# Scattering one dense tile's expert gates with single-element indirect DMAs, and selecting per head over all four tiles

## The chip, the cores and the metric

The kernel runs on one core of a Trainium2 chip. The metric is the device time of one execution in microseconds, the median of several runs. Beside the times there is one profiled execution, from which all rows below come; its own time is given with its span.

## The reference

The reference is a decoder trunk of two layers over 512 tokens of 1024 channels, with 16 meta tokens ahead of them. The first layer mixes by causal pooling, the second by stick-breaking attention; both are followed by a PEER expert network, and this is what the change is about:

```python
s = einsum('bthpc,hpnc->bthpn', q, sub_keys)          # 8 heads, 2 halves, 128 keys each
top_s, top_i = top_k(s, 16)
cand_s = top_s[..., 0, :, None] + top_s[..., 1, None, :]
best_s, best_pos = top_k(cand_s as 256 candidates, 16)
expert = top_i0 * 128 + top_i1 of best_pos             # one of 16384
gate = softmax(best_s)
act = gelu(hx . u[expert]);  y = sum(gate * act * v[expert])
```

So each token takes 8 x 16 experts, and adds their `v` rows, weighted by gate times gelu of the token's product with their `u` rows.

## The kernel before, in words

The 512 tokens are four tiles of 128. In each layer's `peer` (line 255) tiles 0 to 2 are **dense**: every one of the 16384 experts is multiplied with all 384 tokens, in 128 blocks j of 128 experts. A **u step** (`u_parts`, line 307) computes a block's activations with 24 matmuls of 384 columns (line 314; float32 is split into a high and a low half, three products for each of 8 chunks), and the gelu of it (line 321). A **v step** (`v_step`, line 660) multiplies activations by gates (line 678), splits the product and the block's `v` into halves (lines 675 to 683) and adds into six banks `y` with 18 matmuls of 512 columns (line 690). The gates of a block come from a DRAM tensor `gout`, 32 tokens to a group, read by line 673 for four blocks at once. Tile 3 is **gathered**: for each of its 128 expert slots an indirect DMA (`fetch`, line 340) brings one row of `u` and `v` per token, 1 MB in all, VectorE takes the product (line 355), ScalarE its gelu (line 359), VectorE adds the weighted `v` (line 367). In the first layer 16 more such rows serve the meta tokens, behind the others. That makes 144 and 128 rows.

Each layer goes through three stages:

- The **query stage** (loop over heads, line 496): two query projections per head (weights "w"), products with the keys (line 521), and `top16` (line 391) of 8 score vectors per token tile pair on VectorE, five passes each. `select` (line 399) then picks the best 16 of 80 candidates for the gathered tile, one head at a time. `plan` (lines 474 to 487) strews u steps between the heads: it adds WQ_DVE per head to one clock, WQ_PE to another, and inserts u steps of 3.91 us (`ucost`) until the second has caught up.
- The **build stage** (`gate_stream`, line 606): per dense tile one `select` over its eight heads, then `build_gates` (line 553): 32 blocks of 4 tokens, each with four VectorE one-hot passes (lines 593 to 596), 8 matmuls (lines 574 and 576) and one eviction on ScalarE (line 581), stored to `gout`. u steps, in four parts, are put between them by cost (lines 622 to 639). Their activations are spilled to `aout` and read back later.
- The **value stage** (`order`, line 646): the remaining u steps (kept in SBUF), and 128 v steps; while u steps last the order is one u step and two v steps, then v steps alone.

Rows of the gathered tile run through all three by `row_step`, four steps to a row (fetch, product, gelu, update, with up to three rows in flight). The loops call it against a clock: in the value stage

```python
                    tu += ucost
                    while tr < tu and row_step():
                        tr += ROW_PERIOD[layer][1] / 8
                while row_step():
                    pass
```

so a row takes 4 x 13.5/8 = 6.75 us of a clock that runs 3.91 us for each u or v step, and what is left runs after the last of them. Behind it come `finish` for the gathered tile, the last two v steps' matmuls and the additions of `y`.

The tile framework orders each engine's instructions by program order and readiness in a plan made ahead; on the chip each engine takes them in that order. `issue_after` pins: row products and updates stand on VectorE behind the last low half that the program has made before them (`vmark`), their gelus behind the last ScalarE high half (`amark`). The low halves of u and w weights (`load_w`, line 274) are made on GpSimd until the build stage begins and on VectorE from there (`gating`).

After the first layer's experts, `attention` takes the tiles in the order 3, 0, 1, 2 and then the meta tokens (line 765).

## Time and profile before

| | us |
|---|---|
| median of 3 runs | 3131.46 |
| lowest, highest | 3129.51, 3134.83 |
| profiled execution, its own time | 3127.99 |
| its span, first to last instruction | 3126.3 |

The 1.7 us between the last two lie around the program. The median is 3.5 us above the profiled execution. Times in rows are counted from the span's start; PE is TensorE's matmuls, DVE VectorE, ACT ScalarE, POOL GpSimd, SP SyncE. The matmuls of one group overlap, so their mean durations are longer than their distance.

### The profile page before, as it was taken

The numbers are of one execution on the slowest core, as the hardware profiler recorded it, in microseconds if no ns is written. First come the engines' busy times: TensorE is split into PE (matmuls) and PEld (weight loads), VectorE is DVE, ScalarE is ACT, GpSimd is POOL, SyncE is SP. The second block draws the span as 40 slices with busy tenths as digits, with TensorE's granted clock in tenths as the row PEclk, the third lists the DMA queues.
The fourth block names the chain that finished last, engine by engine and source line by source line (L and its number), as shares of the span: only waits on it lengthen the run. The fifth ranks groups of instructions, "written<-read, shape, count | busy, mean of one in ns | idle before, by whom it ended". The sixth has DMA issues, their size and how long they took to land.

```text
span 3126.3 us, 45813 instructions
## 1 busy us (share of the span) xinstructions
PE 2999.0 (96%) x16514; PEld 2671.7 (85%) x16514; DVE 2449.1 (78%) x5636; ACT 1354.3 (43%) x2184; POOL 688.7 (22%) x704
## 2 busy tenths in 40 slices
PE   8988999999999999999999989799999999999999
PEld 7887988988888888879965778798898888888887
DVE  3999998878777778786456469999987777777765
ACT  3443645643333333335455334354655333333333
POOL 3431311111111111114245244222110111111100
PEclk9999999999999999999999999999999999999999
DMA  3435877799989899762100344477878998989875
GB/s 134 179 121 202 282 265 265 274 360 329 338 312 321 314 329 329 273 245 90 55 1 1 108 177 144 158 262 269 303 253 326 358 314 321 331 308 333 307 250 164
DMA packets 286708, 758.52 MB, mean 243 GB/s; under 512 B 23184, under 2 KB 176784, under 8 KB 248336
## 3 DMA queue, kind: packets, MB, share of 16 engines
q1 hardware_dynamic: 222544, 390.92, 36.8%
q0 software_dynamic: 39168, 285.23, 24.9%
q10 hardware_dynamic: 24768, 79.44, 6.6%
q8 instruction: 129, 2.11, 0.3%
q14 instruction: 99, 0.81, 0.1%
HBM read 673.99 MB, written 81.53 MB: 242 GB/s over the span
## 4 chain that ended last, share of the span: by engine, by line
PE 77%; DVE 16%; DMA 3%; ACT 2%; issue 1%; POOL 0%; SPq 0%; DVEq 0%; ACTq 0%; POOLq 0%
PE y L690 31%; PE psu L314 27%; PE pg L574 3%; PE pg L576 3%; PE pp L124 2%; PE pp L125 2%; PE pp L123 2%; DVE mr L395 1%; DVE prod L355 1%; DVE w_lo L281 1%; DMA gt<-gout 1%; DVE ti L397 1%; DVE hx L367 1%; DMA w<-in_peer_ut_dram 1%; DVE ti L394 1%
## 5 line engine op out<-in xcount | busy, mean ns | idle before, releaser
L343 POOL DMA_INDIRECT row<-in_peer_uv_dram,ei x272 | 383.3, 1409 | 1833.1 <-DVE hx L367 1481.9
L314 PE MATMUL psu<-n_hi,w_lo 128*128 128x384 f32 x2048 | 701.5, 343 | 42.4 <-DVE w_lo L281 39.9
L314 PE MATMUL psu<-n_hi,w_hi 128*128 128x384 f32 x2048 | 720.4, 352 | 11.5 <-ACT ac L321 7.2
L314 PE MATMUL psu<-n_lo,w_hi 128*128 128x384 f32 x2048 | 703.0, 343 | 0.6 <-DVE n_lo L118 0.6
L279 ACT ACTIVATE w_hi<-w 128x1024 fp32r<-128x1024 f32 x288 | 305.6, 1062 | 467.7 <-PE psu L314 373.2
L690 PE MATMUL y<-v_lo,wt_hi 128*128 128x512 f32 x1536 | 473.6, 390 | 1.6 <-DVE v_lo L676 1.6
L690 PE MATMUL y<-v_hi,wt_hi 128*128 128x512 f32 x1536 | 473.8, 390 | 0.5 <-ACT v_hi L675 0.5
L690 PE MATMUL y<-v_hi,wt_lo 128*128 128x512 f32 x1536 | 473.6, 389 | 0.0
L314 PEld LDWEIGHTS psu<-n_hi,w_lo 128*128 128x128 f32 x2048 | 394.0, 192 | 49.0 <-DVE w_lo L281 45.8
L314 PEld LDWEIGHTS psu<-n_hi,w_hi 128*128 128x128 f32 x2048 | 395.4, 193 | 17.8 <-ACT ac L321 7.5
L314 PEld LDWEIGHTS psu<-n_lo,w_hi 128*128 128x128 f32 x2048 | 394.0, 192 | 5.5 <-DVE n_lo L118 1.1
L682 ACT ACTIVATE wt_hi<-wt 128x384 fp32r<-128x384 f32 x256 | 134.3, 525 | 574.0 <-PE y L690 295.5
L683 DVE TENSOR_TENSOR wt_lo<-wt,wt_hi 128x384 fp32r<-128x384 f32 x256 | 142.5, 557 | 264.3 <-ACT wt_hi L682 264.3
L281 DVE TENSOR_TENSOR w_lo<-w,w_hi 128x1024 fp32r<-128x1024 f32 x228 | 278.2, 1221 | 83.2 <-ACT w_hi L279 82.6
L690 PEld LDWEIGHTS y<-v_lo,wt_hi 128*128 128x128 f32 x1536 | 288.1, 188 | 63.3 <-DVE v_lo L676 2.9
L690 PEld LDWEIGHTS y<-v_hi,wt_lo 128*128 128x128 f32 x1536 | 288.3, 188 | 60.4
L355 DVE SCALAR_TENSOR_TENSOR prod<-row,hnat 128x1024 bf16<-128x1024 f32 x272 | 337.7, 1241 | 0.6 <-DMA row<-in_peer_uv_dram,ei 0.5
L367 DVE SCALAR_TENSOR_TENSOR hx<-row,gwt,hx 128x1024 f32<-128x1024 f32 x256 | 334.5, 1307 | 2.1
L690 PEld LDWEIGHTS y<-v_hi,wt_hi 128*128 128x128 f32 x1536 | 286.8, 188 | 52.8 <-ACT v_hi L675 0.9
L676 DVE TENSOR_TENSOR v_lo<-v,v_hi 128x1024 fp32r<-128x1024 f32 x256 | 312.2, 1219 | 5.4 <-ACT v_hi L675 5.2
L581 ACT ACTIVATE stage<-pg 128x512 f32<-128x512 f32 x192 | 216.9, 1137 | 149.2 <-PE pg L576 146.3
L675 ACT ACTIVATE v_hi<-v 128x1024 fp32r<-128x1024 f32 x256 | 270.8, 1058 | 10.6 <-DMA v<-in_peer_uv_dram 9.5
(313 smaller groups left out, 4695.0 us busy)
## 6 DMA issues: line engine op xcount, KB each, us to landing
w<-in_peer_ut_dram SPq DMA_DIRECT2D x256, 512.0 KB, 5.9
v<-in_peer_uv_dram SPq DMA_DIRECT2D x256, 512.0 KB, 6.1
gout<-stage ACTq DMA_DIRECT2D x24, 2048.0 KB, 8.4
gt<-gout SPq DMA_DIRECT2D x64, 768.0 KB, 10.2
aout<-ac ACTq DMA_DIRECT2D x148, 192.0 KB, 4.0
ac<-aout SPq DMA_DIRECT2D x148, 192.0 KB, 5.9
w<-in_peer_wq_dram SPq DMA_DIRECT2D x32, 512.0 KB, 3.4
wn<-in_w_kv_dram SPq DMA_DIRECT2D x8, 1024.0 KB, 5.5
```

The source lines that it names most:

```text
L279: amark.append(sc.activation(whi, w, AF.Copy))
L281: vmark.append(v.tensor_sub(wlo, w, whi.bitcast(F32)))
L314: m = pin(pe.matmul(ps[:, :ND], a[:, k, :], b[:, k, c0:c0 + ND], start=st, stop=en))
L343: gp.indirect_dma_start(out=row, out_offset=None, in_=peer_uv, in_offset=bass.IndirectOffsetOnAxis(ap=item[1], axis=0))
L355: v.scalar_tensor_tensor(prod, row[:, :D], 1.0, hn_nat[i], ALU.mult, ALU.mult, accum_out=dot)
L367: v.scalar_tensor_tensor(acc, row[:, D:], wt, acc, ALU.mult, ALU.add)
L581: sc.activation(stage[:, :, o:o + TG].rearrange("p j t -> p t j"), pg, AF.Copy, scale=1.0 / GSCALE)
L675: amark.append(sc.activation(vhi, v32, AF.Copy))
L676: vmark.append(v.tensor_sub(vlo, v32, vhi.bitcast(F32)))
L682: sc.activation(whi, wt, AF.Copy)
L683: vmark.append(v.tensor_sub(wlo, wt, whi.bitcast(F32)))
L690: pe.matmul(y[n][half], wp[:, ts], vq[:, half * 512:(half + 1) * 512], start=st, stop=en)
```

## The change

The gates of dense tile 2 (`NS` = 1 tile) are no longer built. Their tensor `gout` is cleared ahead of time by four DMAs of 2 MB per layer, and each head's 16 gates per token are added into it by 16 indirect DMAs of one element per partition, issued on GpSimd; a head's scatters wait for those of the head before, and row fetches are kept behind the scatters that were issued before them. Tiles 0 and 1 (`BUILT` = 2) are built as before, into a tensor of their own, so a gate load is two DMAs. `select` runs once per head over all four tiles, in the query stage. All low halves are made on VectorE. The pacing is new: 41 us per head in the query stage's plan, one built block after three parts of a u step, and one row step per 4.5 us of the clock in the build stage; per head four row steps (eight at the last).

```diff
-DVE_SLACK = 1.08
-ROW_PERIOD = ((18.0, 13.5), (18.0, 13.5))
-WQ_DVE = (19.0, 19.0)
-WQ_PE = (15.5, 12.5)
+BUILT = 2
+ROW_PERIOD = (13.0, 13.5)
+ROW_B = 36.0
+WQ_DVE = 41.0
+PACE = 3
+WQ_PE = (15.5, 14.5)
-QUIET = 16
...
+    def clear_gates(layer, part, parts):
+
+        g = gouts[layer].rearrange("(p c f) o -> p c (f o)", p=P, f=512)
+        n = NK * NS * P // 512 // parts
+        cleared[layer].append(sc.dma_start(g[:, part * n:(part + 1) * n, :],
+                                           zero.unsqueeze(1).to_broadcast([P, n, 512])))
...
             pre(NT)
             pre(0)
+            clear_gates(0, 0, 4)
             fold()
             for i in range(1, NT):
                 pre(i)
+                clear_gates(0, i, 4)
...
-                if gating[0]:
-                    vmark.append(v.tensor_sub(wlo, w, whi.bitcast(F32)))
-                else:
-                    gp.tensor_sub(wlo, w, whi.bitcast(F32))
+                vmark.append(v.tensor_sub(wlo, w, whi.bitcast(F32)))
...
+            def scatter(count):
+                for _ in range(min(count, len(to_scatter))):
+                    h, n, at, gate = to_scatter.pop(0)
+                    x = gp.indirect_dma_start(out=gout, out_offset=bass.IndirectOffsetOnAxis(ap=at, axis=0),
+                                              in_=gate, in_offset=None, compute_op=ALU.add)
+                    if issued:
+                        after(x, issued[0], sync=False)
+                    issued.append(x)
+                    earlier = placed[n, h - 1] if h else cleared[layer]
+                    for e in earlier:
+                        after(x, e)
...
                 def fetch():
...
+                    for y in issued:
+                        after(x, y, sync=False)
+                    issued[:] = [x]
...
                         while len(plan) > 1 and plan[-1][0] == "u":
                             u_step(plan.pop()[1], True, plan[-1])
                             j0 += 1
+                        i1, i2, gate = select(qp, gr, f"h{h}", tv, ti, NT)
+                        gates_out(h, i1, i2, gate)
+                        for dst, src in zip(picked, (i1, i2, gate)):
+                            v.tensor_copy(dst[:, :, h * TK:(h + 1) * TK],
+                                          src[:, :BUILT * TK].rearrange("p (n q) -> p n q", q=TK))
+                        scatter(NS * TK)
+                        for _ in range(4 if h < H - 1 else 8):
+                            row_step()
                         for i in gathered:
-                            res = []
-                            for _ in select(qp, gr, f"g{i}_{h}", tv[i][:, h:h + 1], ti[i][:, h:h + 1], 1, res):
-                                pass
-                            gather_rows(i, h, *res, TK, hx[i], False)
-                        while tr < tq and row_step():
-                            tr += ROW_PERIOD[layer][0] / 8
+                            of = slice(i * TK, (i + 1) * TK)
+                            gather_rows(i, h, i1[:, of], i2[:, of], gate[:, of], TK, hx[i], False)
...
+                def part():
+
+                    nonlocal parts, done, tu, tr
+                    parts += 1
+                    tu += ucost / UPARTS
+                    if parts % PACE == 0 and done < total:
+                        next(blocks, None)
+                        done += 1
+                    while tr < tu and row_step():
+                        tr += ROW_B / 8
+
+                while done < total:
+                    for _ in u_parts(j0, True, ("u", j0 + 1)):
+                        part()
+                    part()
+                    j0 += 1
...
-                        gts[jg] = vp.tile([P, NB, JG, TB], F32, name="gt", bufs=3)
-                        sy.dma_start(gts[jg], gout[:, :, jg * JG:(jg + 1) * JG, :])
+                        gts[jg] = vp.tile([P, nd * NB, JG, TB], F32, name="gt", bufs=3)
+                        js = slice(jg * JG, (jg + 1) * JG)
+                        sy.dma_start(gts[jg][:, :BUILT * NB], gbuilt[layer][:, :, js, :])
+                        x = sy.dma_start(gts[jg][:, BUILT * NB:], gates[:, :, js, :])
...
                     while tr < tu and row_step():
-                        tr += ROW_PERIOD[layer][1] / 8
+                        tr += ROW_PERIOD[layer] / 8
                 while row_step():
                     pass
...
                 with tc.issue_after(last.ins):
+                    for part in range(4):
+                        clear_gates(1, part, 4)
```

## Rows read from the trace of the kernel before

**Rows 1.** The page: busy time of each engine, its share of the span, instructions.
```profile
PE 2999.0 (96%) x16514; PEld 2671.7 (85%) x16514; DVE 2449.1 (78%) x5636; ACT 1354.3 (43%) x2184; POOL 688.7 (22%) x704
```

**Rows 2.** Three stages of either layer: engines' busy time (instructions), clock, DMA share, GB/s.
```profile
59.00:234.00 175.00, 154.54 (x1114) 150.70 (x1113) 151.38 (x754) 71.66 (x130) 71.83 (x36) 0.95 0.42 145
234.00:640.00 406.00, 378.02 (x2338) 357.11 (x2337) 370.69 (x1016) 214.23 (x276) 79.98 (x33) 0.97 0.72 258
640.00:1400.00 760.00, 757.97 (x3627) 665.32 (x3628) 602.17 (x865) 290.45 (x477) 115.98 (x105) 1.00 0.89 317
1797.00:1990.00 193.00, 172.63 (x862) 151.69 (x861) 160.35 (x771) 77.38 (x108) 85.43 (x41) 0.96 0.44 156
1990.00:2380.00 390.00, 366.22 (x2272) 346.44 (x2271) 357.60 (x938) 207.63 (x269) 69.39 (x32) 0.97 0.73 261
2380.00:3122.00 742.00, 739.71 (x3528) 647.79 (x3528) 562.27 (x800) 279.45 (x448) 97.72 (x86) 1.00 0.86 303
```

**Rows 3.** The chain that ended last: shares by line, then pieces (start, length).
```profile
by line: PE y L690 31.1%; PE psu L314 27.3%; PE pg L574 2.7%; PE pg L576 2.6%; PE pp L124 2.2%; PE pp L125 2.2%; PE pp L123 2.2%; issue 1.5%; DVE mr L395 1.3%; DVE prod L355 1.2%; DVE w_lo L281 1.2%; DMA gt<-gout 1.0%; DVE ti L397 0.9%; DVE
...
306.66 4.23 PE psu L314 x24
...
2991.12 130.36 PE y L690 x575
```

**Rows 4.** TensorE in order of time, second layer's query stage: start, length.
```profile
1954.66 1.60 PE L521 MATMUL ps<-keys,qt 128*128 128x128 f32 x12
...
1965.74 0.39 PE L123 MATMUL psu<-n_hi,w_hi 128*128 128x512 f32 x1
...
1968.30 0.39 PE L125 MATMUL psu<-n_hi,w_lo 128*128 128x512 f32 x1
```

**Rows 5.** The page's groups: matmuls that wait for a low half.
```profile
L314 PE MATMUL psu<-n_hi,w_lo 128*128 128x384 f32 x2048 | 701.5, 343 | 42.4 <-DVE w_lo L281 39.9
```

**Rows 6.** VectorE in order of time, one head's eight key selections, second layer.
```profile
1892.63 0.48 DVE L393 MAX8 tv<-s 128x8 f32<-128x128 f32 x2
...
1902.42 0.18 DVE L436 CAST tib<-ti 128x32 bf16<-128x32 uint32 x1
```

**Rows 7.** VectorE groups: a selection pass over eight heads; the low halves.
```profile
L445 DVE TENSOR_REDUCE gdi<-oh 128x128 f32<-128x2048 bf16 x12 | 27.3, 2278 | 0.0
...
L281 DVE TENSOR_TENSOR w_lo<-w,w_hi 128x1024 fp32r<-128x1024 f32 x228 | 278.2, 1221 | 83.2 <-ACT w_hi L279 82.6
```

**Rows 8.** Row fetches on GpSimd, first layer's build stage: ns min/median/max.
```profile
L343 POOL DMA_INDIRECT row<-in_peer_uv_dram,ei x32: 939/1928/6507, 254.6 to 635.5; - x32
```

**Rows 9.** Row fetches on GpSimd, first layer's value stage: ns, then us to landing.
```profile
L343 POOL DMA_INDIRECT row<-in_peer_uv_dram,ei x101: 939/948/2150, 645.4 to 1362.9; - x101
...
DMA to landing us min/median/max: 5.6/8.7/11.4
```

**Rows 10.** Stretches: start, densest transfers, v steps with rows, attention.
```profile
0.00:50.00 50.00, 39.41 (x226) 35.31 (x227) 21.56 (x42) 20.52 (x36) 19.97 (x92) 0.97 0.45 148
650.00:700.00 50.00, 49.56 (x240) 43.46 (x239) 40.29 (x61) 18.96 (x33) 9.56 (x7) 1.00 1.03 385
1304.00:1363.00 59.00, 57.98 (x255) 47.37 (x254) 51.09 (x76) 22.55 (x37) 7.14 (x8) 1.00 0.90 320
1550.00:1600.00 50.00, 48.48 (x327) 40.96 (x326) 20.72 (x52) 21.43 (x53) 13.34 (x42) 1.00 0.00 1
```

**Rows 11.** DMA issues: activations spilled, KB each, us to landing.
```profile
aout<-ac ACTq DMA_DIRECT2D x148, 192.0 KB, 4.0
```

**Rows 12.** Rows in the first layer's build stage: VectorE, GpSimd busy (instructions).
```profile
234.00:640.00 406.00, 78.57 (x94) 79.19 (x32) 0.97 0.72 258
```

**Rows 13.** The page's groups: VectorE's two passes of a row.
```profile
L355 DVE SCALAR_TENSOR_TENSOR prod<-row,hnat 128x1024 bf16<-128x1024 f32 x272 | 337.7, 1241 | 0.6 <-DMA row<-in_peer_uv_dram,ei 0.5
...
L367 DVE SCALAR_TENSOR_TENSOR hx<-row,gwt,hx 128x1024 f32<-128x1024 f32 x256 | 334.5, 1307 | 2.1
```

**Rows 14.** TensorE where attention begins: start, length, idle before.
```profile
1402.40 1.09 PE L115 MATMUL pt<-ident,xn 128*128 128x128 f32 x8 [1.50 <-DVE xn L108]
```

More of the change, by code (lines that the diff above doesn't have):

```diff
@@ L84, in trunk_kernel @@
     sy.dma_start(hx[0], x[0, :P, :])
+    dense = [i for i in range(NT) if i not in GATHERED]
+    nd = len(dense)
+    assert dense == list(range(nd))
+    ND = nd * P
+    NB = P // TB
+    NS = nd - BUILT
+    gbuilt = [dram.tile([P, BUILT * NB, NK, TB], F32, name=f"gbuilt{layer}") for layer in range(2)]
+    gouts = [dram.tile([P * NS * NB * NK * TB, 1], F32, name=f"gout{layer}") for layer in range(2)]
+    cleared = [[], []]
+    def clear_gates(layer, part, parts):
[3 more added lines that the diff above has]
+                                           zero.unsqueeze(1).to_broadcast([P, n, 512])))
     n_hi = const([P, KC, S + NM], F32R, "n_hi")
@@ L256, in peer @@
         gathered = list(GATHERED)
-        dense = [i for i in range(NT) if i not in gathered]
-        nd = len(dense)
-        c0 = dense[0] * P
-        assert dense == list(range(dense[0], dense[0] + nd))
-        ND = nd * P
-        NB = ND // TB
-        gout = dram.tile([P, NB, NK, TB], F32, name=f"gout{layer}")
+        gout = gouts[layer]
         aout = [dram.tile([P, ND], F32, name=f"aout{layer}_{j}") for j in range(NK)]
@@ L313, in u_parts @@
                                          (wlo, hi, False, k == KC - 1)):
[L314 removed]
+                        m = pe.matmul(ps[:, :ND], a[:, k, :], b[:, k, :ND], start=st, stop=en)
                         n += 1
@@ L327, in u_step, with gates_out, after @@
                 return drained(u_parts(j, spill, following))
+            to_scatter = []
+            placed = {}
+            issued = []
+            def gates_out(h, i1, i2, gate):
+                ds = slice(BUILT * TK, nd * TK)
+                ef = gr.tile([P, NS, TK], F32, name="gf", bufs=2)
+                at = gr.tile([P, NS * TK], I32, name=f"at{h}")
+                v.scalar_tensor_tensor(ef, i1[:, ds].rearrange("p (n q) -> p n q", q=TK), float(TB),
+                                       tok[:, :NS].unsqueeze(2).to_broadcast([P, NS, TK]), ALU.mult, ALU.add)
+                v.scalar_tensor_tensor(at, i2[:, ds], float(NS * NB * NK * TB), ef.rearrange("p n q -> p (n q)"),
+                                       ALU.mult, ALU.add)
+                to_scatter.extend((h, n, at[:, n * TK + q:n * TK + q + 1],
+                                   gate[:, (BUILT + n) * TK + q:(BUILT + n) * TK + q + 1])
+                                  for n in range(NS) for q in range(TK))
+            def after(x, y, sync=True):
+                kind = mybir.DependencyClass.Sync if sync else mybir.DependencyClass.NoSync
+                tc.add_manual_dep(x.ins, y.ins.name, mybir.DependencyInfo(kind, mybir.DependencyReason.DATA),
+                                  reason="gates")
+            def scatter(count):
[9 more added lines that the diff above has]
+                        after(x, e)
+                    tc.declare_no_dep(x.ins, group=f"gates{layer}", keep=[e.ins for e in earlier],
+                                      reason="one head's slots of a token are distinct experts")
+                    tc.add_to_no_dep_group(f"gates{layer}", x.ins)
+                    placed.setdefault((n, h), []).append(x)
             def gather_rows(i, h, i1, i2, gate, ns, acc, first):
@@ L638, in peer @@
-                if steps:
-                    drained(steps)
+                    for n in range(BUILT):
+                        yield from build_gates(n, *(t[:, n, :] for t in picked))
+                blocks = gate_stream()
+                total = BUILT * P // TG
+                done = parts = 0
+                tu = tr = 0.0
+                def part():
[7 more added lines that the diff above has]
+                        tr += ROW_B / 8
```

108 lines of the change are left out of this document (42 added, 66 removed).

## The prediction

> **What bounds it now.** I read the busy shares first: TensorE 96%, VectorE 78% [rows 1]. These are averages, so next the stages. In both value stages TensorE is busy without a gap, 757.97 of 760 us and 739.71 of 742, at full clock; in the query and build stages it is not, the clock is granted at 0.95 to 0.97, and VectorE is busy for 86 to 92% [rows 2]. To see what is lost there I price TensorE's work by its distances: a u step takes 4.23 us, 18 matmuls of a v step 130.36 / 575 x 18 = 4.08 us [rows 3]; a one-hot matmul (2.7% + 2.6% of 3126.3 us) / 1536 = 0.108 us [rows 3], so a block of eight 0.87 us. The projections go at (1968.30 - 1965.74) / 11 = 0.233 us, 384 of them 89 us; twelve key products take 1.6 us, a layer's 128 some 16 us [rows 4]. With that, 105 us a layer for both (the first layer's projections are a little wider; I leave it).
>
> The pacing arithmetic gives 72 u steps ahead of the value stage in the first layer and 76 in the second, in sum the 148 spilled activations of the trace [rows 11]. So query and build stages hold 72 x 4.23 + 96 x 0.87 + 105 = 493 us of TensorE work in 581 us, and 510 in 583: **88 and 73 us lost**. What ends TensorE's waits in u steps is VectorE's low half, 39.9 of 42.4 us [rows 5]; the rest is clock and waits for selections. The value stages: 56 x 4.23 + 128 x 4.08 = 759 us in 760, 742 in 742. Nothing is lost there.
>
> **The change part by part.**
>
> **Blocks not built.** 32 blocks a layer fewer: 28 us of TensorE, 56 us for both layers, and 32 x 4 VectorE passes with them.
>
> **u steps moved forward.** The plan's new constants give 53 and 55 u steps between the heads, two ahead of them, and 64 blocks x 3 parts / 4 = 48 in the build stage: 103 and 105 ahead of the value stage. TensorE's work does not change by this. It is 103 x 4.23 + 64 x 0.87 + 105 = 596 us and 605 us up to the value stage, and 25 x 4.23 + 128 x 4.08 = 628 us and 620 us in it; 1224 and 1225 us a layer against 1341 and 1325 us now. If nothing were lost, that would be **-217 us**: the 161 us lost today and the 56 us of blocks.
>
> **What the new stages lose.** VectorE per head: eight key selections in (1902.42 - 1892.63) = 9.8 us [rows 6]; a selection over four tiles, half of one over eight heads (two one-hot halves with a reduce of 2278 ns each [rows 7] and passes like it), some 15 us; two low halves 2.4 us [rows 7], a row 2.6 us. That is 30 us, 240 us in all, and 53 low halves of 1.22 us make it 305 us, under TensorE's 105 + 55 x 4.23 = 338 us. So TensorE sets the query stage, but tightly: two buffers of low halves, and the third u step of a head has its low half behind 9.8 us of key selections, so I take 4 us a head, 30 us a layer. In the build stage VectorE has 64 x 1.7 + 48 x 1.22 + ten rows = 194 us beside TensorE's 259; I take 8 us for its start. 38 us a layer, **+76 us**. The bounds are 0 (TensorE's floor) and today's 88 and 73.
>
> **Low halves off GpSimd.** 60 passes move from GpSimd to VectorE, whose share of them is counted above; GpSimd's time is on no path there.
>
> **Scatters.** 128 a layer on GpSimd, 16 per head. No row shows an accumulating DMA; the nearest is a row fetch, also 128 descriptors: 0.95 us in the value stage [rows 9], median 1.93 and at most 6.51 us in the build stage [rows 8]. I take 1.5 us, as VectorE's work in the query stage lies between those of the two: 24 us a head, beside 45 us of TensorE and VectorE work, so 0 on the path. Behind a waiting scatter stand the row fetches, one per head, with two more rows in flight; the wait for the head before is for work 45 us old. If that cover went, 16 x 6.51 = 104 us a head would show. The build stage's fetches are delayed in the same way: the trace has that already, the fetch waits while VectorE is dense [rows 8, 9].
>
> **Clears.** Eight DMAs of 2 MB. The second layer's lie in attention, where transfers stand at 0.00 [rows 10]: 0. The first layer's lie in the first 50 us, beside the loads, at a share of 0.45 [rows 10]. At 385 GB/s all four take 22 us: between 0 and that, I take **+3 us**, as half the transfers' time is free.
>
> **More activations read back.** 208 instead of 148. So 78 and 82 v steps now stand without a u step, each with 0.9 MB of loads, and 0.6 of a row. With rows beside them such steps lost 59 - 57.98 = 1.0 us in 59 at 320 GB/s; 385 GB/s was moved in the densest stretch [rows 10], and the new demand is 1.5 MB / 4.08 us = 374 GB/s. I take 8 us a layer, **+16 us**; the bounds are 0 and 0.5 us a step.
>
> **Rows left over.** This decides. Rows follow the pacing clock: the old constants give 30 fetches in the first layer's build stage, and the trace has 32 [rows 12]. The new constants give, in steps of a quarter row, 32 in the query stage, 188 / 4.5 = 42 in the build stage, and 153 x 3.91 / 1.625 = 369 in the value stage: 443 of 576. In the second layer 32 + 42 + 351 = 425 of 512. So **33 and 22 rows** are left when the last v step has been issued; before it was none. They are pinned behind that step's low half, so VectorE takes them while TensorE has two v steps left. A row costs VectorE 1.24 + 1.31 us [rows 13], at least 2.6; three in flight with a landing of 8.7 (at most 11.4) us [rows 9] give 2.9 to 3.8. I take 3.0. Second layer: 22 x 3.0 - 7 = 59 us, bare at the end (bounds 50 and 77). First layer: 33 x 3.0 - 7 = 92 us; attention starts today 3 us behind the experts [rows 14], with tile 3, and the meta tokens' rows come last; some of its first projections could go beside them, I take 8 us off: 84 (bounds 47, if tile 3's 18 rows alone hold it, and 118). **+143 us**.
>
> **Sum.** -217 + 76 + 3 + 16 + 143 = +21 us on the profiled execution's 3128.0: 3149. The median stands 3.5 us higher, so I give 3151.
>
> **The rivals.**
>
> *The stages fill up* (faster). If the new query stage loses no more than the value stages do, 5 us a layer, 66 us go from the sum: 3085. It decides below 22 us lost a layer. For it: VectorE has only 0.9 of TensorE's work there, and TensorE would hold the clock. Against: today's stages never came near. 27%.
>
> *The value stage runs out of transfers* (slower yet). 160 bare v steps at 0.5 us more: 3215. For it: 374 of 385 GB/s. Against: [rows 10] lost 2%. 13%.
>
> *GpSimd holds the heads.* A fetch takes 0.95 us beside the value stage's VectorE and up to 6.51 us beside the build stage's [rows 8, 9], so VectorE's passes can keep GpSimd from its descriptors. At 4 us a scatter (between the build stage's median and its longest) a head takes 64 us, 19 more: 16 x 19 = 304, so 3455. Against: the query stage has few passes like the build stage's. 6%. The Trainium skill (SBUF — State Buffer, section "SBUF: two separate sides") states such a lock: while VectorE is in a two-port mode, GpSimd cannot write descriptors. By that rule the time goes this way if selection runs in such modes; the trace's 6.51 us beside 0.95 agrees.
>
> *The leftover rows are not left*, since the plan issues them earlier than their place: -143, 3008. Against: the pins, and a trace that follows the clock. 6%.
>
> **How the numbers follow.** My forecast has 48%, from 3115 to 3190. Faster and slower both hold a good part; the likeliest case's own range is that one. For eight in ten the range goes from 3070, in the first rival, to 3230, past the second. What this kernel's measurement can tell from no change is 0.2%, 6 us. Faster by more: the first and last rivals and a small part of the forecast, 0.36; within: 0.12; slower: 0.52.
>
> **What would show it.** Right: 103 and 105 spills; 33 and 22 row updates after the last low half of a v step, near 3 us apart, with TensorE idle at the span's end for about 55 us; a query stage near 370 us and a build stage near 267. Wrong: no bare rows at the end; u steps over 5 us apart through the heads; scatters near 3 us; v steps at 4.5 us.

## The result, and the profile after

The changed kernel takes 3393.07 us (median of 4 runs, 3384.23 to 3401.21), the kernel before beside it 3132.84 us: a ratio of 1.083, 95% interval 1.080 to 1.086. The forecast was 3151 us, 3115 to 3190 for its own case and 3070 to 3230 for eight in ten. The sign was right, but the loss is 260 us where the forecast's was 20. The profiled execution took 3397.1 us, 3395.4 of it its span.

The page's busy shares, to set against [rows 1]:

```profile
PE 2967.4 (87%) x15996; PEld 2630.7 (77%) x15996; DVE 2384.2 (70%) x5346; ACT 1269.9 (37%) x2098; POOL 924.7 (27%) x901
```

All engines but GpSimd are less busy than before, in a span 269 us longer: time has become waiting. The stages of the changed kernel, in the columns of [rows 2] (stretch, length, busy time with instructions of PE, PEld, DVE, ACT and POOL, clock, DMA share, GB/s): start, query, build, value, bare rows; then the second layer's four:

```profile
0.00:77.00 77.00, 49.21 (x271) 43.67 (x272) 29.32 (x53) 23.45 (x41) 19.14 (x93) 0.93 0.61 215
77.00:500.00 423.00, 367.30 (x2297) 360.31 (x2296) 294.24 (x1210) 146.79 (x232) 203.89 (x126) 0.94 0.54 136
500.00:810.00 310.00, 280.15 (x1687) 264.63 (x1686) 184.01 (x369) 139.01 (x178) 37.71 (x25) 0.94 0.63 219
810.00:1442.00 632.00, 616.54 (x2803) 521.17 (x2802) 517.51 (x760) 236.84 (x390) 104.13 (x90) 0.99 0.95 342
1442.00:1548.00 106.00, 9.88 (x38) 7.12 (x37) 92.95 (x146) 10.87 (x41) 51.17 (x35) 0.56 0.85 314
1962.00:2380.00 418.00, 362.00 (x1898) 336.21 (x1897) 287.98 (x1162) 142.53 (x198) 198.50 (x122) 0.94 0.54 138
2380.00:2693.00 313.00, 281.19 (x1721) 266.21 (x1720) 183.23 (x363) 141.13 (x181) 42.63 (x30) 0.96 0.64 219
2693.00:3318.00 625.00, 606.12 (x2751) 511.89 (x2750) 505.64 (x740) 232.99 (x381) 98.39 (x86) 0.99 0.94 338
3318.00:3392.00 74.00, 8.19 (x36) 6.19 (x34) 63.89 (x100) 5.64 (x24) 28.61 (x20) 0.57 0.81 305
```

Stage by stage against the forecast's terms (before: 59 us of start, 395 of attention between 1402 and 1797):

| | forecast | measured |
|---|---|---|
| start | 59 + 3 | 77 |
| query and build, beyond TensorE's 596 and 605 | 38 and 38 | 733 - 596 = 137, 731 - 605 = 126 |
| value stages | 636 and 628 | 632 and 625 |
| rows left over | 84 and 59 | 106 and 74 |
| attention | 395 | 1962 - 1548 = 414 |

The differences are 15 + 187 - 7 + 37 + 19 = 251 us; the profiled execution stands 3397.1 - 3149 = 248 above the sum. Three quarters of the miss lie in the query and build stages.

Where TensorE waits there, the page's groups say, to set against [rows 5]; below it are the row products, which were not late before [rows 13]:

```profile
L330 PE MATMUL psu<-n_hi,w_lo 128*128 128x384 f32 x2048 | 710.2, 347 | 159.1 <-DVE w_lo L305 158.8
...
L412 DVE SCALAR_TENSOR_TENSOR prod<-row,hnat 128x1024 bf16<-128x1024 f32 x272 | 331.4, 1218 | 111.6 <-DMA row<-in_peer_uv_dram,ei 111.6
```

The wait for VectorE's low halves has grown from 39.9 to 158.8 us, and VectorE now waits 111.6 us for rows. Its longest wait, in order of time (start, length, engine, line, idle before and what ended it), on GpSimd, on VectorE and on TensorE:

```profile
186.13 1.54 POOL L370 DMA_INDIRECT gout<-h1gate,at  x1 [0.31 <-issue]
187.98 1.54 POOL L370 DMA_INDIRECT gout<-h1gate,at  x1 [0.30 <-issue]
189.83 1.01 POOL L397 DMA_INDIRECT row<-in_peer_uv_dram,ei  x1 [0.31 <-issue]
...
195.41 1.23 DVE L412 SCALAR_TENSOR_TENSOR prod<-row,hnat 128x1024 bf16<-128x1024 f32 x1 [33.17 <-DMA row<-in_peer_uv_dram,ei]
...
196.56 2.36 DVE L305 TENSOR_TENSOR w_lo<-w,w_hi 128x1024 fp32r<-128x1024 f32 x2
...
197.84 0.69 PE L330 MATMUL psu<-n_hi,w_lo 128*128 128x384 f32 x1 [28.97 <-DVE w_lo L305]
```

GpSimd issues the 32 scatters of heads 0 and 1 from 125.1 to 189.5 us, and the first row fetch stands behind them. Its product is next on VectorE, which takes instructions in order, so two low halves stand behind the product and TensorE stands behind these. The next head's copy of the scores comes 119 us after this one's (111.9 to 230.5); the plan has 14 u steps and two projections there, 71 us. The second layer has the same gap, 118 us. After it the heads go at (455.2 - 230.5) / 5 = 44.9 us, as forecast.

The build stage begins in the same way: the last head's 16 scatters, the row fetch behind them, and on VectorE and TensorE:

```profile
529.35 1.23 DVE L412 SCALAR_TENSOR_TENSOR prod<-row,hnat 128x1024 bf16<-128x1024 f32 x1 [18.50 <-DMA row<-in_peer_uv_dram,ei]
...
532.44 0.69 PE L330 MATMUL psu<-n_hi,w_lo 128*128 128x384 f32 x1 [15.29 <-DVE w_lo L305]
```

With the same two places of the second layer, VectorE waits 33.2 + 18.5 + 31.7 + 22.0 = 105 us for a row at four places, and TensorE idles 29.0 + 15.3 + 27.5 + 17.7 = 90 us behind them.

The scatters themselves, of heads 0 and 7 in both layers (ns: least, median, most; first and last start):

```profile
L370 POOL DMA_INDIRECT gout<-h0gate,at x32: 1537/1550/2302, 125.1 to 2041.0; - x32
...
L370 POOL DMA_INDIRECT gout<-h7gate,at x32: 1542/1546/5548, 487.0 to 2407.5; - x32
```

The median is 1.55 us against the 1.5 taken; with the 0.30 between them, one per 1.85 us.

The bare rows of the first layer, as groups of the stretch 1442 to 1548, which answer to [rows 13]:

```profile
L412 DVE SCALAR_TENSOR_TENSOR prod<-row,hnat 128x1024 bf16<-128x1024 f32 x34 | 41.4, 1218 | 1.8 <-DMA row<-in_peer_uv_dram,ei 1.8
L424 DVE SCALAR_TENSOR_TENSOR hx<-row,gwt,hx 128x1024 f32<-128x1024 f32 x19 | 24.4, 1282 | 0.4
L424 DVE SCALAR_TENSOR_TENSOR gain<-row,gwt,gain 128x1024 f32<-128x1024 f32 x15 | 19.3, 1285 | 0.5
...
L422 DVE TENSOR_SCALAR gain<-row,gwt 128x1024 f32<-128x1024 f32 x1 | 0.8, 793 | 0.0
```

35 row updates (19 + 15, and the first of the meta tokens) follow the last low half of a v step there and 23 in the second layer, 2.9 and 3.1 us apart (33 and 22 at 3.0 were forecast). TensorE idles under them. VectorE waits only 1.8 us for rows, and 8.6 us for their gelus, so it is VectorE's own passes that make the chain.

### The profile page after: what moved, and what is told of

The parts are those of the page before. It is cut to its first block, busy times and chain, and to the rows that moved or that the text cites. A ratio compares the mean times of both kernels' runs of the same rounds, so it can differ in the third digit from the quotient of the medians.

```text
span 3395.4 us, 45035 instructions
## 1 busy us (share of the span) xinstructions
PE 2967.4 (87%) x15996; PEld 2630.7 (77%) x15996; DVE 2384.2 (70%) x5346; ACT 1269.9 (37%) x2098; POOL 924.7 (27%) x901
## 3 DMA queue, kind: packets, MB, share of 16 engines
q0 software_dynamic: 76032, 285.38, 25.7%
## 5 line engine op out<-in xcount | busy, mean ns | idle before, releaser
L330 PE MATMUL psu<-n_hi,w_lo 128*128 128x384 f32 x2048 | 710.2, 347 | 159.1 <-DVE w_lo L305 158.8
L397 POOL DMA_INDIRECT row<-in_peer_uv_dram,ei x272 | 332.7, 1223 | 1674.2 <-DVE hx L424 1581.7
L305 DVE TENSOR_TENSOR w_lo<-w,w_hi 128x1024 fp32r<-128x1024 f32 x288 | 351.0, 1220 | 242.2 <-ACT w_hi L304 241.7
L412 DVE SCALAR_TENSOR_TENSOR prod<-row,hnat 128x1024 bf16<-128x1024 f32 x272 | 331.4, 1218 | 111.6 <-DMA row<-in_peer_uv_dram,ei 111.6
L637 ACT ACTIVATE stage<-pg 128x512 f32<-128x512 f32 x128 | 143.6, 1129 | 170.4 <-PE pg L634 170.1
```

The source lines that it names most:

```text
L305: vmark.append(v.tensor_sub(wlo, w, whi.bitcast(F32)))
L330: m = pe.matmul(ps[:, :ND], a[:, k, :], b[:, k, :ND], start=st, stop=en)
L397: x = gp.indirect_dma_start(out=row, out_offset=None, in_=peer_uv, in_offset=bass.IndirectOffsetOnAxis(ap=item[1], axis=0))
L412: v.scalar_tensor_tensor(prod, row[:, :D], 1.0, hn_nat[i], ALU.mult, ALU.mult, accum_out=dot)
L637: sc.activation(stage[:, :, o:o + TG].rearrange("p j t -> p t j"), pg, AF.Copy, scale=1.0 / GSCALE)
```

## The experiments

All times are medians of 4 runs (10 for the kernel before with more buffers), each beside the kernel before on the same chip, which stood between 3132 and 3135 us.

**No rows left over.**

```diff
-ROW_PERIOD = (13.0, 13.5)
+ROW_PERIOD = (9.4, 10.7)
```

> The row periods go from 13.0 and 13.5 to 9.4 and 10.7 in the value stage, so that by the plan's arithmetic no row is left behind the last v step; nothing else changes. Theory (the tail is work pinned too late): the bare rows, 106 us after the first layer's value stage and 74 us after the second's, go, and VectorE, busy for 518 of 632 us in the value stage, takes 33 and 22 rows of 2.6 us more there, 86 and 57 us, which just fit: the value stages grow by 10 to 30 us each; attention starts at full clock again, 10 us more. 3393 - 180 - 10 + 20 to 60 = 3225 to 3265. Rival (value stages short of transfers): the DMA share is 0.95 there already and a row brings 1 MB; 33 MB and 22 MB more at 342 GB/s are 96 and 64 us, so the stages grow by as much as the tails had, and the time stays over 3340.

3298.52 us, 95 less: between the two. The tails are gone. The value stages, and ScalarE's longest wait in the first one (850 to 1480 us):

```profile
806.00:1483.00 677.00, 638.89 (x2809) 527.62 (x2809) 592.76 (x899) 240.62 (x422) 167.27 (x121) 0.98 1.00 369
...
2635.00:3285.00 650.00, 623.02 (x2761) 514.25 (x2760) 554.92 (x832) 239.57 (x404) 137.48 (x105) 0.98 0.98 357
```

```profile
L727 ACT ACTIVATE v_hi<-v 128x1024 fp32r<-128x1024 f32 x121 | 128.1, 1059 | 106.1 <-DMA v<-in_peer_uv_dram 91.8 <-PE y L742 11.5 <-issue 2.6
```

They have grown by 45 and 25 us, with the DMA share at 1.00 and 0.98 and v loads that come late: of 180 us of tail, 70 come back there, and some 8 us a layer of TensorE's last products, which had run under the tail, stand bare again. That the late loads make the 70 us is read from the trace and not shown: TensorE's idle time in the two stages is 38 and 27 us, against 15 and 19 in the changed kernel, the rest is longer busy time, and VectorE is busy for 593 of 677 us. The tails hold rows that the value stages can carry only in part.

**Rows first.**

```diff
-                        scatter(NS * TK)
                         for _ in range(4 if h < H - 1 else 8):
                             row_step()
+                        scatter(NS * TK)
```

> Per head, the row steps come ahead of the head's 16 scatters in program order instead of behind them; the same instructions otherwise. Theory (the loss of the query stages is the first row fetches that stand behind 32 scatters on GpSimd while VectorE, in order, waits 33 us at the first row product): the 47 us gap between heads 1 and 2 closes to 10 us or less, in both layers; the build stages keep their wait, since their fetches still stand behind the last head's scatters. 3393 - 70 to 95 = 3298 to 3323. Rival (scatters as such slow the heads, through the DMA rings or the port that GpSimd shares with VectorE): the gap only moves to a later head, and the time stays within 20 us of 3393.

3318.12 us, 75 less. The gap is 99 us instead of 118; the first row product waits less (in order of time):

```profile
162.20 1.23 DVE L412 SCALAR_TENSOR_TENSOR prod<-row,hnat 128x1024 bf16<-128x1024 f32 x1 [10.93 <-DMA row<-in_peer_uv_dram,ei]
```

Only head 0's 16 scatters stand before the first fetch now. The gap was to close to 81 us or less, and it did not. The time lies in the theory's range only because the build stage has shortened too (310 to 289 us; no row product waits there any more), which I had not expected. The same instructions in another order give 75 us.

**No scatters.**

```diff
-                        scatter(NS * TK)
+                        to_scatter.clear()
...
-                            for e in placed[n, H - 1]:
+                            for e in cleared[layer]:
```

> The scatters are left out, so tile 2's gates stay zero and its part of the sum is missing; their indices are still computed, the clears and all loads stay. Theory (what scatters cost is only the place in GpSimd's queue ahead of the row fetches): the gap in the heads goes, 45 us a layer, and the wait at the build stage's start, 15 us a layer: 3393 - 110 to 135 = 3258 to 3283, and steady heads stay at 45.6 us. Rival (scatters also slow VectorE or the transfers while they run): steady heads become faster than 45.6 us, towards 41, another 30 us a layer, near 3210.

3294.27 us, 99 less, 11 short of what was expected. Query and build stages of both layers:

```profile
76.00:465.00 389.00, 362.37 (x2293) 355.71 (x2292) 292.47 (x1212) 146.55 (x232) 13.91 (x11) 0.97 0.46 155
465.00:757.00 292.00, 277.72 (x1701) 262.86 (x1701) 184.03 (x367) 140.23 (x179) 16.20 (x13) 0.98 0.63 222
1907.00:2295.00 388.00, 360.11 (x1887) 334.64 (x1886) 287.47 (x1162) 142.08 (x199) 11.35 (x11) 0.96 0.46 152
2295.00:2588.00 293.00, 278.86 (x1719) 264.31 (x1718) 183.42 (x362) 140.70 (x178) 15.87 (x13) 0.98 0.65 230
```

The four are 1362 us instead of 1464, 102 less: the whole gain is there. The steady heads go at 44.7 us with no scatter beside them against 44.9 with 16 each, so the rival, that running scatters slow VectorE or the transfers, is out. What remains of the gap is 87 us, against 71 us of TensorE's work.

**Clears from another queue.**

```diff
-        cleared[layer].append(sc.dma_start(
+        cleared[layer].append(sy.dma_start(
```

> The eight clearing transfers are issued from SyncE's queue instead of ScalarE's. Theory (the clears cost time because ScalarE stands at their issue, 3.5 and 5.4 us in attention, and because they stand ahead of other transfers at the start): the start is shorter by 5 to 15 us and attention by 5 to 9: 3393 - 10 to 24 = 3369 to 3383. Rival (8 MB of clears beside the first loads take their time from whichever queue): no change beyond 5 us, or slower, as SyncE's queue holds the x loads.

3373.68 us, 19 less. ScalarE's waits for x at the start, with the clears on its own queue and then on SyncE's:

```profile
L117 ACT ACTIVATE junk<-hx 128x1024 bf16<-128x1024 f32 x7 | 7.4, 1057 | 24.6 <-DMA hx<-in_x_dram 17.2 <-DVE hx L264 7.2
```

```profile
L117 ACT ACTIVATE junk<-hx 128x1024 bf16<-128x1024 f32 x7 | 7.4, 1054 | 5.8 <-DVE hx L264 5.5 <-DMA hx<-in_x_dram 0.2
```

The first clear had been issued at 1.5 us, beside the loads of x; from SyncE it goes at 13.8. In attention ScalarE had stood 10 us at the second layer's four issues (1733.8 to 1743.8). From SyncE these four go out at 61.7 to 85.8 us, long before attention, so the run changes their place as well as their queue.

**All three, rows spread over build and value stage.**

```diff
-ROW_PERIOD = (13.0, 13.5)
-ROW_B = 36.0
+ROW_PERIOD = (10.5, 12.0)
+ROW_B = 18.0
```

(with rows first and the clears on SyncE's queue)

> Row steps ahead of the scatters, clears from SyncE's queue, and rows paced so that none is left: 1.125 row periods of the build stage's clock become half as long (36.0 to 18.0, 10 more rows there), 10.5 and 12.0 in the value stages (113 and 97 rows there instead of 92 and 88). From the runs of each: 3318 with rows first, less 19 for the clears, less the tails and attention's slow start, 190, plus 25 and 10 for the value stages (45 for 35 rows more in the first, in the run with all leftover rows there). Theory A (a row in the build stage takes the place of a low half on VectorE, TensorE then idles about 2 us and runs some us at half clock, so a row costs about 3 us there): 20 rows, 60 us: 3204. Theory B (rows in the build stage are free, VectorE being busy for 184 of 310 us): 3145, that is level with the kernel before.

(The figure 1.125 in this text means nothing; the constants are 36.0 and 18.0.) 3195.29 us, near theory A's 3204, but not by its terms. From the first to the last eviction of a block the build stages take 277 and 279 us, 7 more than with rows first: 10 rows cost 0.7 us each there, not 3. The value stages took 664 and 638 us, 35 and 11 more than with rows first, for 21 and 9 rows more by the plan. So theory A falls on its own point, and B's sum is 50 us short: 25 of it are the value stages' 46 instead of 35 and the build stages' 14, the rest I put down to the 190 us for tails and attention, which was too much.

**Tile 2 built as well.**

```diff
-BUILT = 2
-PACE = 3
+BUILT = 3
+PACE = 2
```

(and no clears, indices and scatters)

> Tile 2 is built from one-hots like the other two, without clears and scatters; per-head selection, all low halves on VectorE and the new pacing stay, and two parts of a u step go ahead of a block instead of three, so that again 103 and 105 u steps stand ahead of the value stage. Theory (the scatters cost more than the 32 blocks that they spare): less 99 for the scatters (the run without them), less 19 for the clears, plus 2 x 32 x 0.87 = 56 for the blocks: 3331, and VectorE in the build stage, 96 x 1.7 + 48 x 1.22 + 26 = 248 us beside TensorE's 287, adds up to 30: 3320 to 3361. Rival (building is the dearer way, as the one-hot passes push low halves back): 3393 or more.

3328.97 us: as the theory had it. In the setting of the changed kernel, scattering a tile, with its clears, costs 64 us more than building it.

**More buffers for one-hot products** (with rows first).

```diff
-                        ab = gb.tile([P, 3, NK, TG], F16, name="ab", bufs=GLAG + 1)
+                        ab = gb.tile([P, 3, NK, TG], F16, name="ab", bufs=GLAG + 3)
```

> Rows first as before, and two more buffers for the one-hot products of a block, with no other edit. Theory (the build stage loses 30 us where 8 were expected because VectorE stands at a one-hot pass that waits for TensorE to free the product buffer, 81 us a stage, with the next low half behind it): with more buffers the passes run ahead, the low halves come earlier, and each build stage gives back 10 to 25 us: 3268 to 3298, against 3318 with rows first. Rival (the low half is late because a row's product stands ahead of it, or because of its own two buffers): within 8 us of 3318.

3327.70 us: no gain, and the theory falls as to the cure. VectorE still waits for TensorE at a one-hot pass, 75.7 us of a build stage against 78.3, and TensorE for low halves, 13.0 us against 12.4: I read it as VectorE filling the two buffers more and waiting again, with the low half still behind the pass.

**Low halves of the query stage back on GpSimd** (with rows first).

```diff
-                vmark.append(v.tensor_sub(wlo, w, whi.bitcast(F32)))
+                if gating[0]:
+                    vmark.append(v.tensor_sub(wlo, w, whi.bitcast(F32)))
+                else:
+                    gp.tensor_sub(wlo, w, whi.bitcast(F32))
...
+                gating[0] = True
```

> Rows first as before, and the low halves of the query stages go back to GpSimd, where one takes 2.43 us. Theory (GpSimd has no room for them beside the scatters: per head 16 x 1.85 + 8.6 x 2.43 + 1.3 = 52 us against 45.6 of a head now, and a low half stands behind scatters that wait for a selection): query stages 30 to 100 us longer each, 3380 to 3520. Rival (VectorE's own load is what makes the heads lose 4 us each, and 65 us less of it is a gain): 3270 to 3318.

3684.75 us, 367 more, well past the theory's own figure. Busy shares of 77 to 650 us, and the projections' wait in that stretch:

```profile
77.00:650.00 573.00, 374.17 (x2264) 366.47 (x2263) 251.91 (x1110) 141.60 (x226) 363.27 (x194) 0.82 0.39 101
```

```profile
L563 PE MATMUL psu<-n_hi,w_lo 128*128 128x264 f32 x128 | 41.1, 321 | 145.3 <-POOL w_lo L309 145.3
```

Heads take about 74 us though GpSimd is busy for only 363 of 573: a low half stands behind 16 scatters, and TensorE has nothing until it comes. With two buffers, moving the low halves to VectorE is a part that the scatters need, not one beside them.

**Three buffers of weights, loaded two steps ahead** (on the version at 3195).

```diff
-            def weight(key, following=None):
-                for kk in (key, following):
+            def weight(key, *following):
+                for kk in (key, *following):
...
-                wlo = up.tile([P, KC, P], F32R, name="w_lo", bufs=2)
+                wlo = up.tile([P, KC, P], F32R, name="w_lo", bufs=3)
...
-                            w, whi, wlo = weight(plan.pop(), plan[-1])
+                            w, whi, wlo = weight(plan.pop(), plan[-1], plan[-2])
```

(the same for w_hi and for the u steps; w32 and wt one buffer fewer)

> The version with rows first, clears from SyncE's queue and rows paced to the end (3195), with three buffers instead of two for the high and the low halves of u and w weights, and the load of a weight made two steps ahead of its use instead of one; to make room the raw weights have two buffers instead of three and the gated activations one instead of two. Theory (what is still lost in the heads and the build stage is a low half that waits for one of two buffers and then stands on VectorE behind key selections or a row): steady heads go from 44.8 to 41 to 43 us, the gap between heads 1 and 2 from 98 to about 85, each build stage from 277 to 260 to 270: 3195 - 40 to 80 = 3115 to 3155. Rival (the low half is placed late by VectorE's order as such, whatever the buffers, or VectorE itself sets the heads): within 12 us of 3195.

3089.39 us, 106 less, more than expected, and below the kernel before: 0.985 (0.983 to 0.987). The steady heads go at (404.3 - 200.5) / 5 = 40.8 us, TensorE's own time, and the build stages are 273 and 283 us (295 and 299 without). The gap between heads 1 and 2 did not shrink as expected: 103 us.

**u steps between heads 0 and 1 too.**

```diff
-                        while tu < td and h > 0:
+                        while tu < td:
```

> As the run with three weight buffers, and u steps are also put between heads 0 and 1, where the plan had none (13 stood between heads 1 and 2). Theory (between heads 1 and 2 TensorE idled 10 us at a stretch, and ran at half clock around it, since VectorE had two heads of selections before it and nothing was left for TensorE): 10 to 18 us a layer less than in the run with three buffers, 20 to 36 in all. Rival (the same VectorE work only comes due at another place): within 8 us of it.

(The plan has 14 u steps between heads 1 and 2, not 13.) 3043.45 us, 46 less again: 0.971 of the kernel before (0.969 to 0.973), the best version here. Stages (query, build, value of either layer) and the group of low-half waits, for this kernel:

```profile
63.00:425.00 362.00, 355.93 (x2303) 353.18 (x2302) 294.57 (x1209) 148.99 (x235) 217.93 (x127) 1.00 0.69 191
425.00:697.00 272.00, 269.79 (x1701) 257.94 (x1701) 208.09 (x414) 141.99 (x188) 56.07 (x37) 1.00 0.80 283
697.00:1338.00 641.00, 618.76 (x2780) 515.11 (x2780) 561.21 (x844) 239.68 (x408) 122.36 (x109) 0.99 1.01 372
1752.00:2114.00 362.00, 356.63 (x1941) 335.73 (x1940) 291.56 (x1166) 144.75 (x202) 209.00 (x126) 1.00 0.62 165
2114.00:2395.00 281.00, 272.16 (x1705) 260.68 (x1704) 205.35 (x401) 142.24 (x189) 61.67 (x40) 0.98 0.79 277
2395.00:3020.00 625.00, 604.61 (x2734) 507.96 (x2733) 524.96 (x781) 233.66 (x388) 107.31 (x93) 0.99 0.98 354
```

```profile
L330 PE MATMUL psu<-n_hi,w_lo 128*128 128x384 f32 x2048 | 691.8, 338 | 4.5 <-DVE w_lo L305 4.5
```

The wait for low halves is 4.5 us in all, the clock of the query stages 1.00. Query and build stages hold 362 + 272 = 634 and 643 us, 38 us a layer over TensorE's 596 and 605. That is the forecast's figure, but by luck: it had the 38 us as waits, and TensorE is busy here for all but 8 and 14 us of them. 15 us a layer of the rest are 3.6 u steps of the value stage that already run in these stretches (2558 and 2608 matmuls, 24 to a step, where 103 and 105 steps were priced).

**Three weight buffers, tile 2 built.** The edit of the run with tile 2 built, on the version at 3089 (with no scatters, the order of rows and scatters falls away).

> As the run with three weight buffers, but tile 2 is built from one-hots, with no clears and scatters, and two parts of a u step ahead of a block. Theory (with the row fetches out from behind them the scatters cost 11 us a layer and the clears about 5 to 10 in all, less than the 28 us of blocks that they spare): 15 to 35 us slower than the run with three buffers. Rival (the scatters cost as much as the blocks even so): level with it or faster.

3111.96 us, 23 more than 3089.39 (ratios to the kernel before 0.993, 0.991 to 0.995, and 0.985, 0.983 to 0.987). In this setting, with only head 0's scatters ahead of the first fetch and the clears on SyncE's queue, scatters are cheaper than 32 blocks. The runs of each account for the turn: of the 64 us by which scattering was dearer, the order takes 75 and the clears' place 19, which leaves it 30 us cheaper by the sum.

**The kernel before with the three buffers.** The same edit, on the kernel before; four small buffers of it one fewer for room.

> The kernel before, with three buffers for high and low halves and weights loaded two steps ahead (raw weights and gated activations one buffer fewer, and four small buffers of the build stage one fewer, to make room). Theory (its query and build stages are set by VectorE, busy there for 86 to 92%, so buffers give it little; what gains from them is the changed kernel, whose VectorE has time left): 3135 - 0 to 40 = 3095 to 3135, so that the changed kernel in its best setting, 3043, stays ahead. Rival (its 42 us of waits for low halves and the clock that dips with them all go): 3030 to 3070, and the lead of the changed kernel is that of the buffers alone.

3141.03 us, 1.002 of the kernel before (1.001 to 1.003): nothing gained, and 6 us over the theory's end. The waits for low halves did go, from 39.9 us [rows 5] to 16.3:

```profile
L314 PE MATMUL psu<-n_hi,w_lo 128*128 128x384 f32 x2048 | 699.7, 342 | 16.4 <-DVE w_lo L281 16.3
```

but the key products' waits for queries rose from 24.4 to 49.0 us. I read it as VectorE setting these stages, whatever is stored ahead; that the four smaller buffers cost what the three larger ones gave is not excluded. The lead of the changed kernel's best version is not that of the buffers alone.

**The changed kernel with the three buffers alone.**

> The changed kernel as it stands, with only the three buffers and the look-ahead of two. Theory (the buffers give about what they gave to the mended version, 106 us, while the first rows' wait behind the scatters, the clears and the tails stay): 3393 - 80 to 110 = 3283 to 3313, still slower than before by 5%. Rival (with a low half more in store TensorE also rides over part of the wait for the first rows): below 3270.

3279.15 us, 114 less, just under the theory's figures and 4.8% over the kernel before. VectorE's wait for rows in the query stage (77 to 475 us) stays, 29.5 of it for the row itself:

```profile
L412 DVE SCALAR_TENSOR_TENSOR prod<-row,hnat 128x1024 bf16<-128x1024 f32 x8 | 9.7, 1218 | 32.4 <-DMA row<-in_peer_uv_dram,ei 29.5 <-issue 2.9
```

**More rows in the build stage** (on the best version).

```diff
-ROW_PERIOD = (10.5, 12.0)
-ROW_B = 18.0
+ROW_PERIOD = (11.0, 12.5)
+ROW_B = 14.0
```

> As the run with u steps between heads 0 and 1 (3043), with 6 rows a layer more in the build stage (14.0 instead of 18.0) and as many fewer in the value stages (11.0 and 12.5 instead of 10.5 and 12.0). Theory (the first layer's value stage stands at the limit of transfers, 642 us at 380 to 390 GB/s, and the build stages have VectorE and transfers to spare): value stages 8 to 16 and 0 to 5 us shorter, build stages 0 to 5 longer: 3025 to 3043. Rival (a row in the build stage costs TensorE 3 us): 3045 to 3070.

3061.40 us, 18 more: the theory falls, though not for the rival's reason alone. The build stages, from first to last eviction, are 10 and 7 us longer, and the first value stage is longer as well, 664 instead of 649 us (first high half of v to the last matmul), with five rows fewer in it; ScalarE waits 56 us for v loads there, 60 before. So its length is not set by the bytes alone. TensorE's waits for a gated activation's high half rose from 9.7 to 17.8 us; what makes them late was not tried.

## Why the prediction was wrong

**Right.** The plan's arithmetic: 208 spills, 103 and 105; 35 and 23 bare rows about 3 us apart. The price of a scatter. The steady heads, 4 us each over TensorE's time, and three buffers took these 4 us away. The value stages came within 4 us, though 2.4 u steps (10 us) a layer had run ahead of the line that I drew. Three slips decide nothing: 3149 + 3.5 is 3152.5, 1.5 MB in 4.08 us are 368 GB/s, and VectorE's share in [rows 2] is 83 to 92% (160.35 of 193 us).

**The step that failed** is the scatters' "0 on the path". It weighed GpSimd's 24 us a head against a head of 45 us, with rows in flight to cover a late fetch. That holds from head 2 on. At head 1 no row is in flight: three fetches and the first product are issued at once, behind 32 scatters, and VectorE's low halves stand behind that product. The step asked whether GpSimd has time enough, and not what stands behind the first fetch on GpSimd, and then on VectorE and on TensorE. The last head's scatters hold the first fetch of the build stage in the same way. TensorE idles 90 us at these four places; with the scatters out 99 us go, with another order alone 75; 0 was taken. The upper bound for what the new stages lose, the 88 and 73 us of the kernel before, was no bound either: the change brings a wait that those stages did not have.

**The new stages' loss** without the scatters was 1362 - 1201 = 161 us where 76 were taken; 20 of it are u steps of the value stage that run ahead (2540 and 2568 matmuls). Two things were left out. Heads 0 and 1 have no u steps between them, so two heads of selections come due at once: in the run without scatters TensorE idled 9.6 us for a low half at head 1, and the stretch 120 to 140 us had a clock of 0.74. And the build stage has more than a late start: at eight places of 292 us TensorE idles 1.4 to 2.4 us, 14 us in all. One of them, in that run, on VectorE and on TensorE:

```profile
683.74 0.42 DVE L649 TENSOR_TENSOR ab<-iota_x,sl 128x512 f16<-128x512 f16 x1 [2.55 <-PE pg L634]
...
684.76 1.22 DVE L305 TENSOR_TENSOR w_lo<-w,w_hi 128x1024 fp32r<-128x1024 f32 x1
...
686.03 0.45 PE L330 MATMUL psu<-n_hi,w_lo 128*128 128x384 f32 x1 [1.61 <-DVE w_lo L305]
```

VectorE has time, 2.55 us of it ahead of these passes, but spends it at a one-hot pass that waits for TensorE to free a buffer; the low half that TensorE needs next stands behind. The forecast compared loads (194 us of VectorE beside 259 of TensorE) and saw no wait there. Three buffers and u steps between heads 0 and 1 took nearly all of TensorE's waits away (8 us are left in the first layer and 14 in the second). That the buffers do it by letting low halves run ahead of such passes is read from the traces; no run had the buffers without the longer look-ahead.

**The clears**, 3 taken, cost 18 us at the start (first copy of scores at 98.1 us, at 79.7 in the run with tile 2 built, which has no clears) and 7 in attention. The step costed the bytes, and "transfers stand at 0.00" in attention is true of bytes, but not of ScalarE, which stands at the issue; at the start the loads of x came late beside the first clears. Sent from SyncE, the second layer's ahead of attention, they give 19 us back.

**The leftover rows**: the mechanism held; 143 taken, 180 measured. The 8 us that attention was to save at the first layer's tail were not saved, two rows more were left in the first layer and one in the second, and the first layer's tail ran its 106 us to the end. About 7 of attention's 19 us stay also without clears and tails (1382.6 to 1809.6 us in the run with three buffers and tile 2 built, 1399.2 to 1819.1 before, from the last work of the experts to the next layer's first scores). Before, tile 3's last row was done 13 us ahead of the last matmul of the experts, and there it is not; I read it as tile 3 being ready later, and it was not tried.

**Of the rivals**, "GpSimd holds the heads" was the nearest in time (3455) and wrong in cause: it had scatters at 4 us and all heads late. They took 1.55 us, and two places a layer were late, the first heads and the build stage's start.

The Trainium skill (SBUF — State Buffer, section "SBUF: two separate sides") states that GpSimd cannot write descriptors while VectorE runs an operation in a two-port mode. In which mode the passes of the heads run, no trace here shows. The trace has a median of 1.55 us over 256 scatters; 14 took more than 2.5 us, the longest 5.55, and each of these ran beside a low half on VectorE. All that is above 1.55 comes to some 34 us of GpSimd's time in both layers, so here it decides nothing.

"The stages fill up" did not happen in the changed kernel, which lost 137 and 126 us there; the version with u steps between heads 0 and 1 comes near it. "The value stage runs out of transfers" did not happen, since the tails held the rows. When the rows were moved in, the value stages grew by 70 us at 369 and 357 GB/s, but with fewer rows in it a stage was not shorter, so transfers alone are not shown to set it. "The leftover rows are not left" is out.

## What to carry to other kernels

When work is added to a queue, how full it gets in a period is the second question; the first is what comes next on it at the start, before anything is in flight, and what stands behind that on each engine in turn. In-order engines that feed each other small steps gained from a buffer and a step of look-ahead more where neither of them had all the work; in the kernel before, with VectorE busy for most of these stages, it brought nothing. A change that is 8% slower as it stands led to a version 3% faster once its order, pacing and buffers fitted it, so a part is priced in the setting that suits it, and its rival in the same. With three buffers tile 2 built gains 0.7% and tile 2 scattered 1.5%, so about half of that gain is not the scatters'. u steps between heads 0 and 1 were tried neither with tile 2 built nor in the kernel before, so how much of the 3% needs the scatters stays open.

## What the hardware showed

An indirect DMA that adds one element per partition costs GpSimd 1.55 us, more than the 0.95 of a row fetch that brings 8 KB to each; it is 1.54 while VectorE stands still (164 to 195 us), so VectorE is not the reason. Nor is the number of packets: GpSimd's queue has 39168 for 272 fetches before and 76032 for 528 fetches and scatters after, 144 each. The reason stays open. Beside VectorE's low halves (1.2 us) some scatters take about 1 us longer. ScalarE stood up to 5.4 us at the issue of one clear of 2 MB.

The clock granted to TensorE has two levels, 1.2 and 2.4 GHz, which stand in the rows as 0.50 and 1.00; a figure between is the mean of a stretch that holds both. After TensorE's idle of 29 us the next 6 us have 0.65. The stretches at the first layer's gap:

```profile
160.00:168.00 8.00, 8.00 (x48) 8.00 (x46) 1.23 (x1) 2.80 (x4) 6.76 (x5) 1.00 0.61 156
168.00:198.00 30.00, 1.03 (x6) 0.71 (x6) 2.59 (x4) 1.44 (x2) 21.06 (x15) 0.56 0.42 85
198.00:204.00 6.00, 6.00 (x24) 6.00 (x25) 0.92 (x1) 0.20 (x1) 0.00 (x0) 0.65 0.80 307
204.00:212.00 8.00, 8.00 (x47) 8.00 (x46) 2.45 (x2) 2.67 (x4) 0.00 (x0) 1.00 0.46 133
```

Short idles were followed by either level. In the run without scatters TensorE idled 1.39 us before 506.4 us, 1.61 us before 686.0 and 1.61 us before 720.8; the stretches from there:

```profile
506.40:510.40 4.00, 3.96 (x14) 3.96 (x15) 1.45 (x2) 0.22 (x2) 0.00 (x0) 0.57 0.60 194
686.00:690.00 4.00, 3.97 (x24) 3.80 (x25) 1.69 (x3) 0.24 (x1) 0.00 (x0) 1.00 0.95 361
720.80:724.80 4.00, 3.96 (x15) 3.96 (x16) 1.45 (x2) 0.00 (x0) 0.00 (x0) 0.63 0.62 175
```

So the length of the idle alone does not tell what the clock does.
